# A two-layer encoder kernel on one core: the output projection's weight blocks are formed in another buffer, and four pieces of work around it change places

## The chip, the core and the metric

The kernel runs on one core of a Trainium2 chip. Its engines have queues of their own and run side by side: TensorE (PE in the profile: matmuls and transposes; PEld is its loading of weights), VectorE (DVE), ScalarE (ACT), GpSimd (POOL) and SyncE (SP, which only issues transfers). An instruction waits in its engine's queue until the semaphores it needs have come; what is queued behind it waits too. The metric is the device time of one execution, in microseconds (us).

## The reference

Two layers, each a gated mixer of three branches on 512 rows of 1024 numbers and then a SwiGLU FFN, all in float32. The part that the change is about:

```python
    merged = (g[:, :, 0] * jnp.einsum('bse,ed->bsd', o_a, w_branch_a[l])
              + g[:, :, 1] * jnp.einsum('bse,ed->bsd', o_b, w_branch_b[l])
              + g[:, :, 2] * jnp.einsum('bse,ed->bsd', o_c, w_branch_c[l]))
    mix = jnp.einsum('bsd,de->bse', merged, w_out[l])
    x = _layer_norm(DEEPNORM_ALPHA * x + mix, ln1_g[l], ln1_b[l])

    u = jnp.einsum('bsd,df->bsf', x, w_ffn_in[l])
    u_gate, u_up = jnp.split(u, 2, axis=-1)
    ffn = jnp.einsum('bsf,fd->bsd', jax.nn.silu(u_gate) * u_up, w_ffn_out[l])
    x = _layer_norm(DEEPNORM_ALPHA * x + ffn, ln2_g[l], ln2_b[l])
```

## The kernel before

**Products of pairs.** Each float32 operand is carried as a high part (a cast to float32r, on ACT) and a low part (the float32 number minus the high part, on DVE). One product is three matmuls onto one bank of PSUM: high by high, high by low, low by high (`mm3`, L121 to L124). For weights, `wh` and `wl` are the two parts and `st` is the float32 buffer that a transfer fills. There are four `st` buffers (NSTAGE), three `wh` and three `wl` (AHEAD), used in turn: a cast into `wh` waits until PE has finished the block that had the buffer three blocks earlier.

**Seven products instead of eight.** The large projections are done by Strassen-Winograd: the weights in four quarters W11, W12, W21, W22, the activations too, and seven products with sums of quarters on both sides. The kernel names the seven weight blocks m1, m2, y, v, x, g, h. A block has 1024 KB and is multiplied in two halves j (128 rows of the result each) by four k groups by three matmuls: 24 matmuls of 512 columns. The classes `Halves`, `Chain`, `Close`, `Early` and `Late` say how a block's weights come to be; `Staged` (L289) is one block: the cast at L297, the low part at L302. A quarter is added to another either by DVE (`tensor_add`) or by a transfer that POOL issues and that adds to what is in the buffer (`more`, L177). With `later=True` a block makes only its cast at once, and `low()` is called at another place.

**The output projection** (`out_items`, L1210) uses class `Late`. y's weights are W11 + W12, in buffer `a`. v's are W22, in buffer `d`. After v's two parts are made, DVE adds `a` into `d` (L247): these are x's weights. After x's parts, POOL adds W21 into `d` by a transfer (`more`, L282): h's weights. g's are W12 + W22, made by transfers in buffer `c` (`ahead_c`).

The activations of y and x are `s12` (left sums, `Quarters.left`), those of v and g `s43` (right sums, `Quarters.right`), those of m1 and m2 and h the merged rows. There are four such sums, k = 0 to 3, each two subtractions on DVE (L324 and L325, or L334 and L335), one cast on ACT (L108) and one low part on DVE (L114). Those of k = 2 and 3 are made while m2 and y run.

Each product ends in `plus` (L1192), which adds or subtracts its bank to the rows `z` of the residual stream (L1197 for the first addition to a piece of z, L1199 for the others). z has four row tiles t with two halves of 512 columns each. x, g and h go on in m1's banks: PE must not begin g in a bank until x's subtraction has read it, nor h until g's has. m1's and m2's additions are held back in the list `late` and made during v. When both halves of a row tile are complete, `normalise` (L515) computes mean and variance (bn_stats L499, aggregate L517), the reciprocal root on POOL (L520, a power) and the normalised rows (L522, two halves). x completes row tiles 0 and 1, h completes 2 and 3. Then PE transposes the rows (`transposes_of`, L540, into banks `px`), ACT applies gain and bias (L556), and xT's parts (L106, L112) are made from that. They are the activations of the FFN.

**The FFN's opening.** The first items are blocks m1 and m2 of w_ffn_in's first quarter set (`Chain`, object `ffn_opening`), then the plain tiles 16, 17, 18 (`u_ffn`; their weights are `Wt`, with casts and low parts in two halves of 1024 numbers, L154 and L155), then block y.

**What sets the order.** The program is a list of items; an item's weights are fetched (transfer, cast, low part) some items ahead (`run_items`, L585), and other work is put between an item's halves. From the traced program a scheduler with a priority for each instruction makes one order per engine at compile time. `tc.issue_after(ins)` forbids it to put an engine's instructions ahead of `ins` on the same engine; `behind[fn]` lists such instructions for what is fetched while item `fn` begins. Each engine runs its list in order.

Of the kernel before, what the change touches and what calls it, by code (L numbers as in the profile page):

```python
# [56 lines left out]
def trunk(ctx, tc, x_in, xT_in, w_in, ret_norm_g, da_norm_g, lq1, lk1, lq2, lk2, w_a, w_b, w_c, b_merge, w_out,  # L57
          ln1_g, ln1_b, w_ffn_in, w_ffn_out, ln2_g, ln2_b, rel, rope_ret, rope_da, decay, out):
    nc = tc.nc
# [131 lines left out]
    class Chain(Halves):  # L191
# [24 lines left out]
        def x(self):  # L216
            return self.take(1, 0)
# [3 lines left out]

        def v(self):
            return self.block(self.load(1, 1))

        def h(self):
            return self.block(self.__dict__.pop("a"))
# [50 lines left out]
    class Late(Early):  # L277


        def x(self):  # L280
            b = self.block(self.d)
            self.more(self.d, 1, 0)  # L282
            return b

        def h(self):
            self.closing = Staged(self.__dict__.pop("d"), self.kh, later=True)
            return self.closing
# [372 lines left out]
    def layer(l):  # L660
# [7 lines left out]
        v = {}  # L668
# [541 lines left out]
        def out_items():  # L1210
# [5 lines left out]
            def it(name, i, hf, op, last=False, whole=False):  # L1216
                def fn(wt):
                    on = {"x": "m1", "g": "m1", "h": "m1", "v": "y"}.get(name, name)
                    for j in range(2):
# [276 lines left out]
        p, q, r, u = u_fin(0, ffn_opening), u_fin(1, Close), u_fin(2, Close), u_fin(3, Close)  # L1496
        o, w = fout_items(0), fout_items(1)
        for (specs, fn), *groups in [
            (([ffn_opening.m1_high], p["m1"][1]), [], [s_turned(1)]), (p["m2"], [], [s_natural(0)]), (u_ffn(16), [s_x1(0)], [s_x1(1)]),
# [66 lines left out]
```

## Time and profile before

| | us |
|---|---|
| median of 3 runs (lowest, highest) | 1877.56 (1877.21, 1878.15) |
| profiled execution, its own time | 1878.1 |
| its span, first to last instruction | 1876.3 |
| PE busy | 1857.0 (99%) |
| DVE busy | 1392.5 (74%) |
| ACT busy | 989.6 (53%) |
| POOL busy | 129.9 (7%) |

Rows of the profile read: start, duration, engine, line, operation, output<-inputs, shape, and in brackets how long the engine was idle before and what ended that. In the table of waits the three numbers are the total, the number of times and the longest. In the table by stretches each engine has its busy time and its number of instructions, and behind them stand the granted PE clock, the share of the transfer engines and GB/s. Layer 0's output projection runs from about 553 to 596 us of the span, and the FFN's first blocks to 613; layer 1's lie 933.8 us later.

### The profile page before, as it was taken

The page shows a single profiled execution, that of the slowest core. Times are in us where ns is not written, and L with a number is a line of the kernel's source. Part 1 is how long each engine was busy: PE and PEld are TensorE (multiplying, and loading weights), DVE is VectorE, ACT ScalarE, POOL GpSimd, SP SyncE. Part 2 cuts the span into 40 slices and gives each one's busy share as a digit, 9 for nine tenths or more (in the row PEclk, how much of TensorE's full clock was granted, in tenths as well). Part 3 has the DMA queues.
Part 4 walks back from the last instruction along what each step waited for, and adds up shares of the span by engine and source line. Part 5 has one row for each costly group of instructions (what it writes and reads, how often), then busy time and mean ns, then how long its engine had stood idle before and what let it go on. Part 6 is the DMA issues. An engine that isn't in the chain of part 4 may idle for free.

```text
span 1876.3 us, 23363 instructions
## 1 busy us (share of the span) xinstructions
PE 1857.0 (99%) x8772; PEld 1546.9 (82%) x8772; DVE 1392.5 (74%) x2121; ACT 989.6 (53%) x1590; POOL 129.9 (7%) x151
## 2 busy tenths in 40 slices
PE   9999999999999999999999999999999999999998
PEld 7788888888887888888888888888888868888887
DVE  6777756677678776888687777567775887778886
ACT  5545545576545445555354555546665454455540
POOL 2000000000001000010010000000000011000100
PEclk9999999999999999999999999999999999999999
DMA  9685444332457577697486844433325486777871
GB/s 286 177 266 152 123 144 126 90 124 79 129 152 179 157 183 194 184 227 208 135 226 184 256 115 143 154 114 97 112 68 146 136 201 150 197 191 203 203 199 46
DMA packets 235425, 302.89 MB, mean 161 GB/s; under 512 B 8756, under 2 KB 127632, under 8 KB 235312
## 3 DMA queue, kind: packets, MB, share of 16 engines
q1 hardware_dynamic: 205888, 244.09, 40.0%
q0 software_dynamic: 29280, 57.05, 17.6%
q8 instruction: 69, 1.13, 0.2%
q14 instruction: 44, 0.36, 0.1%
q10 hardware_dynamic: 144, 0.26, 0.0%
HBM read 279.29 MB, written 22.07 MB: 161 GB/s over the span
## 4 chain that ended last, share of the span: by engine, by line
PE 88%; DVE 7%; ACT 2%; DMA 2%; issue 1%; POOL 0%; SPq 0%; DVEq 0%; ACTq 0%; POOLq 0%
PE pt L122 14%; PE pt L124 14%; PE pt L123 14%; PE pf L124 13%; PE pf L123 13%; PE pf L122 13%; DVE wl L302 2%; PE ptr L470 1%; ACT wh L297 1%; PE psc L441 1%; PE psc L440 1%; PE pco L983 1%; PE ph L1339 1%; DVE wl L155 1%; DMA xf<-in_xT 1%
## 5 line engine op out<-in xcount | busy, mean ns | idle before, releaser
L302 DVE TENSOR_TENSOR wl<-st,wh 128x2048 fp32r<-128x2048 f32 x140 | 320.2, 2290 | 119.9 <-ACT wh L297 119.3
L122 PE MATMUL pt<-xTh,wh 128*128 128x512 f32 x960 | 376.9, 393 | 1.3 <-ACT wh L154 0.7
L123 PE MATMUL pt<-xTl,wh 128*128 128x512 f32 x960 | 374.1, 390 | 0.4 <-DVE xTl L112 0.3
L124 PE MATMUL pt<-xTh,wl 128*128 128x512 f32 x960 | 374.1, 390 | 0.0
L297 ACT CAST wh<-st 128x2048 fp32r<-128x2048 f32 x140 | 267.1, 1912 | 199.9 <-PE pf L124 86.9
L154 ACT CAST wh<-st 128x1024 fp32r<-128x1024 f32 (+2 forms) x186 | 172.2, 949 | 121.8 <-PE pt L123 61.1
L155 DVE TENSOR_TENSOR wl<-st,wh 128x1024 fp32r<-128x1024 f32 (+2 forms) x186 | 200.6, 1096 | 46.1 <-ACT wh L154 32.4
L122 PEld LDWEIGHTS pt<-xTh,wh 128*128 128x128 f32 x960 | 180.2, 188 | 38.1 <-ACT wh L154 1.1
L124 PEld LDWEIGHTS pt<-xTh,wl 128*128 128x128 f32 x960 | 180.2, 188 | 38.0
L123 PEld LDWEIGHTS pt<-xTl,wh 128*128 128x128 f32 x960 | 180.4, 188 | 37.4 <-DVE xTl L112 0.7
L122 PE MATMUL pf<-wh,xTh 128*128 128x512 f32 x336 | 132.2, 395 | 0.4
L123 PE MATMUL pf<-wl,xTh 128*128 128x512 f32 x336 | 131.7, 392 | 0.6 <-DVE wl L302 0.6
L124 PE MATMUL pf<-wh,xTl 128*128 128x512 f32 x336 | 130.5, 391 | 0.0
L122 PE MATMUL pf<-wh,s43h 128*128 128x512 f32 x256 | 100.3, 393 | 2.0 <-DVE z L1199 2.0
L123 PE MATMUL pf<-wl,s12h 128*128 128x512 f32 x256 | 100.1, 391 | 1.2 <-DVE wl L302 1.2
L122 PE MATMUL pf<-wh,s12h 128*128 128x512 f32 x256 | 100.2, 395 | 0.0
L124 PE MATMUL pf<-wh,s12l 128*128 128x512 f32 x256 | 99.5, 390 | 0.0
L123 PE MATMUL pf<-wl,s43h 128*128 128x512 f32 x256 | 99.4, 390 | 0.0
L124 PE MATMUL pf<-wh,s43l 128*128 128x512 f32 x256 | 99.2, 390 | 0.0
L790 ACT COPY tc<-pf 128x512 f32<-128x512 f32 x84 | 48.5, 590 | 81.5 <-PE pf L124 78.2
L122 PEld LDWEIGHTS pf<-wh,xTh 128*128 128x128 f32 x336 | 63.2, 188 | 15.3 <-ACT xTh L106 1.4
L123 PEld LDWEIGHTS pf<-wl,xTh 128*128 128x128 f32 x336 | 63.4, 189 | 13.8 <-DVE wl L302 1.3
(328 smaller groups left out, 3668.1 us busy)
## 6 DMA issues: line engine op xcount, KB each, us to landing
st<-in_w_in SPq DMA_DIRECT2D x53, 1024.0 KB, 5.6
st<-in_w_ffn_in SPq DMA_DIRECT2D x38, 1024.0 KB, 5.8
st<-in_w_in SPq DMA_DIRECT2D x48, 512.0 KB, 4.8
st<-in_w_ffn_out SPq DMA_DIRECT2D x22, 1024.0 KB, 7.4
st<-in_w_ffn_in POOLq DMA_DIRECT2D x20, 1024.0 KB, 10.2
st<-in_w_ffn_out POOLq DMA_DIRECT2D x16, 1024.0 KB, 8.8
st<-in_w_in POOLq DMA_DIRECT2D x12, 1024.0 KB, 11.1
st<-in_w_ffn_in SPq DMA_DIRECT2D x24, 512.0 KB, 5.7
```

Of the source, the lines that this page charges most:

```text
L122: nc.tensor.matmul(ps, lh, rh, start=start, stop=False, skip_group_check=onto)
L123: nc.tensor.matmul(ps, lh, rl, start=False, stop=False, skip_group_check=onto)
L124: nc.tensor.matmul(ps, ll, rh, start=False, stop=stop, skip_group_check=onto)
L154: return [nc.scalar.copy(self.hi[:, a:b], self.st[:, a:b]), nc.vector.tensor_sub(self.lo[:, a:b], self.st[:, a:b], f(self.hi[:, a:b]))]
L155: nc.vector.tensor_sub(self.lo[:, a:b], self.st[:, a:b], f(self.hi[:, a:b]))]
L297: nc.scalar.copy(self.hi, st)
L302: nc.vector.tensor_sub(self.lo, self.st, f(self.hi))
L440: nc.tensor.matmul(ps[:, :w], self.q[j][:, n], self.k[j][:, :w], start=True, stop=False)
L441: nc.tensor.matmul(ps[:, :w], self.q[j][:, n], self.kl[j][:, :w], start=False, stop=True)
L470: nc.tensor.transpose(ps[:, o + P * (nt - mt):o + P * (nt - mt) + P], E[pk][:, c + P * mt:c + P * mt + P], ident)
L790: nc.scalar.copy(t[to, j], ps)
L983: nc.tensor.matmul(*x, start=mt == 0 and x is hi, stop=mt == NT - 1 and x is hi)
```

## The change

It has four parts, the same in both layers.

1. **x's weights on y's buffer.** `Late.v` adds `d` into `a` and no longer `a` into `d`. x, and then h, take their weights from `a`. The addition reads `d` and overwrites `a`, whose other readers are y's cast and low part.
2. **m2's sums around x.** The four held-back additions of m1 and m2 were made during v, m2's behind the last right sum's low part. Now m1's two and m2's first are made after v's first half, and m2's second after x's first half, behind the vector instruction ahead of x's own subtraction.
3. **g's cast behind the first right sum.** What is fetched when v and x begin stood, on DVE, behind the low part of the last right sum. It stands there still, and on ACT behind the cast of the right sum k = 2.
4. **FFN's second low part behind h.** Block m2 of the FFN makes only its cast when it is fetched; its low part is issued behind h's second addition. What is fetched when the FFN's m1 begins (tile 16's weights) stands, on DVE, behind the last normalisation.

```diff
@@ class Chain
+        def m2_high(self):
+            self.second = Staged(self.load(1, 0), self.kh, later=True)
+            return self.second
+
@@ class Late
+        def v(self):
+            d = self.load(1, 1)
+            b = self.block(d)
+            nc.vector.tensor_add(self.a, self.a, d)
+            return b
+
         def x(self):
-            b = self.block(self.d)
-            self.more(self.d, 1, 0)
+            b = self.block(self.a)
+            self.more(self.a, 1, 0)
             return b
 
+        def y(self):
+            return self.block(self.a)
+
         def h(self):
-            self.closing = Staged(self.__dict__.pop("d"), self.kh, later=True)
+            self.closing = Staged(self.__dict__.pop("a"), self.kh, later=True)
             return self.closing
@@ s_mright
                 mq[k].right(acc.pop(k), acc.pop(k + 4), 0.5)
+                if k == 2:
+                    proj["high"] = last_of(nc.scalar)
                 if k == 3:
-                    proj["sums"] = last_of(nc.vector)
                     for name in ("v", "x"):
-                        behind[proj[name][1]] = [proj["sums"]]
+                        behind[proj[name][1]] = [proj["high"], last_of(nc.vector)]
@@ out_items
-                        if name == "v":
-                            late[j]()
-                            with tc.issue_after(proj["sums"]):
-                                late[2 + j]()
+                        if name == "v" and j == 0:
+                            for _ in range(3):
+                                late.pop(0)()
+                        if name == "x" and j == 0:
+                            with tc.issue_after(last_of(nc.vector, 2)):
+                                late.pop()()
...
                             behind[proj["h"][1]] = [last_of(nc.vector)]
+                        if name == "h" and j == 1:
+                            with tc.issue_after(last_of(nc.vector)):
+                                ffn_opening.second.low()
                         if whole:
                             x1["n"].normalise(t)
+                        if name == "h" and j == 1:
+                            behind[proj["next"]] = [last_of(nc.vector)]
@@ the FFN's items
+        proj["next"] = p["m1"][1]
...
-(p["m2"], [], [s_natural(0)])
+(([ffn_opening.m2_high], p["m2"][1]), [], [s_natural(0)])
```

The number of instructions of each engine stays what it was, and the lists of SP and POOL keep their order. Those of DVE, ACT and PE change in these stretches alone. (After the change, lines behind L222 have other numbers: L302 becomes L315, L297 L310, L1197 L1211, L1199 L1213, L522 L535.)

DVE before, layer 0, while m2 and y run. st_4848 is `a`, st_5147 is `d`; wl_5150 is v's low part, wl_5188 x's; sa_5096 and sa_5103 are the left sums k = 2 and 3; z_4792 and z_4794 take m1's additions:

```order
L324 TENSOR_TENSOR sa_5096<-th_2515,th_3087 128x256
L1197 SCALAR_TENSOR_TENSOR z_4792<-z_4792,pf_5114 128x512
L325 TENSOR_TENSOR sa_5096<-sa_5096,th_2515 128x256
L1197 SCALAR_TENSOR_TENSOR z_4794<-z_4794,pf_5134 128x512
L302 TENSOR_TENSOR wl_5150<-st_5147,wh_5149 128x2048
L114 SCALAR_TENSOR_TENSOR s12l_5100<-sa_5096,s12h_5099 128x512
L324 TENSOR_TENSOR sa_5103<-th_2590,th_3162 128x256
L247 TENSOR_TENSOR st_5147<-st_5147,st_4848 128x2048
L325 TENSOR_TENSOR sa_5103<-sa_5103,th_2590 128x256
L302 TENSOR_TENSOR wl_5188<-st_5147,wh_5187 128x2048
```

The same place after:

```order
L337 TENSOR_TENSOR sa_5096<-th_2515,th_3087 128x256
L287 TENSOR_TENSOR st_4848<-st_4848,st_5147 128x2048
L338 TENSOR_TENSOR sa_5096<-sa_5096,th_2515 128x256
L315 TENSOR_TENSOR wl_5150<-st_5147,wh_5149 128x2048
L114 SCALAR_TENSOR_TENSOR s12l_5100<-sa_5096,s12h_5099 128x512
L337 TENSOR_TENSOR sa_5103<-th_2590,th_3162 128x256
L1211 SCALAR_TENSOR_TENSOR z_4792<-z_4792,pf_5114 128x512
L338 TENSOR_TENSOR sa_5103<-sa_5103,th_2590 128x256
L1211 SCALAR_TENSOR_TENSOR z_4794<-z_4794,pf_5134 128x512
L315 TENSOR_TENSOR wl_5188<-st_4848,wh_5187 128x2048
```

The addition moved ahead of v's low part, and m1's two additions to z moved behind it.

ACT before, from x's cast (wh_5187) over g's (wh_5220) to h's (wh_5256); s43h_5130 and s43h_5170 are the right sums k = 2 and 3:

```order
L297 CAST wh_5187<-st_5147 128x2048
L108 ACTIVATE s12h_5106<-sa_5103 128x512
L297 CAST wh_5220<-st_5007 128x2048
L108 ACTIVATE s43h_5130<-sb_5127 128x512
L108 ACTIVATE s43h_5170<-sb_5167 128x512
L297 CAST wh_5256<-st_5147 128x2048
```

The same place after (h's cast is now wh_5254):

```order
L310 CAST wh_5187<-st_4848 128x2048
L108 ACTIVATE s12h_5106<-sa_5103 128x512
L108 ACTIVATE s43h_5130<-sb_5127 128x512
L310 CAST wh_5220<-st_5007 128x2048
L108 ACTIVATE s43h_5170<-sb_5167 128x512
L310 CAST wh_5254<-st_4848 128x2048
```

g's cast and the first right sum's cast have changed places, and x and h read the other buffer.

DVE before, where h ends and the FFN begins. wl_5313 and wl_5416 are the low parts of the FFN's m1 and m2, wl_5463 that of tile 16; z_4796 and z_4798 take h's two additions; xTl are low parts of the FFN's activations:

```order
L302 TENSOR_TENSOR wl_5313<-st_5310,wh_5312 128x2048
L112 TENSOR_TENSOR xTl_5351<-xf_5352,xTh_5350 128x256
L302 TENSOR_TENSOR wl_5416<-st_5413,wh_5415 128x2048
L112 TENSOR_TENSOR xTl_5357<-xf_5358,xTh_5356 128x256
L1197 SCALAR_TENSOR_TENSOR z_4796<-z_4796,pf_5114 128x512
L1197 SCALAR_TENSOR_TENSOR z_4798<-z_4798,pf_5134 128x512
L499 BN_STATS bn_4810<-z_4796 128x6
L499 BN_STATS bn_4811<-z_4798 128x6
L112 TENSOR_TENSOR xTl_5368<-xf_5369,xTh_5367 128x256
L517 BN_AGGR mv_5433<-bn_4810 128x2
L517 BN_AGGR mv_5454<-bn_4811 128x2
L155 TENSOR_TENSOR wl_5463<-st_5461,wh_5462 128x1024
```

The same place after, from h's second addition (its first stands five rows further ahead, behind the first xTl) to the last normalisation:

```order
L1211 SCALAR_TENSOR_TENSOR z_4798<-z_4798,pf_5134 128x512
L532 TENSOR_SCALAR rs_5434<-mv_5432 128x1
L512 BN_STATS bn_4811<-z_4798 128x6
L535 TENSOR_SCALAR z_4796<-z_4796,mv_5432,rs_5434 128x512
L112 TENSOR_TENSOR xTl_5374<-xf_5375,xTh_5373 128x256
L535 TENSOR_SCALAR z_4797<-z_4797,mv_5432,rs_5434 128x512
L315 TENSOR_TENSOR wl_5416<-st_5413,wh_5415 128x2048
L112 TENSOR_TENSOR xTl_5385<-xf_5386,xTh_5384 128x256
L530 BN_AGGR mv_5454<-bn_4811 128x2
L532 TENSOR_SCALAR rs_5456<-mv_5454 128x1
L535 TENSOR_SCALAR z_4798<-z_4798,mv_5454,rs_5456 128x512
L112 TENSOR_TENSOR xTl_5391<-xf_5392,xTh_5390 128x256
```

h's additions and row tile 2's normalisation moved ahead of m2's low part; row tile 3's normalisation stands behind it, and tile 16's low part behind that.

More of the change, by code (lines that the diff above doesn't have):

```diff
@@ L1496, in layer @@
         p, q, r, u = u_fin(0, ffn_opening), u_fin(1, Close), u_fin(2, Close), u_fin(3, Close)
+        proj["next"] = p["m1"][1]
         o, w = fout_items(0), fout_items(1)
         for (specs, fn), *groups in [
-            (([ffn_opening.m1_high], p["m1"][1]), [], [s_turned(1)]), (p["m2"], [], [s_natural(0)]), (u_ffn(16), [s_x1(0)], [s_x1(1)]),
+            (([ffn_opening.m1_high], p["m1"][1]), [], [s_turned(1)]), (([ffn_opening.m2_high], p["m2"][1]), [], [s_natural(0)]), (u_ffn(16), [s_x1(0)], [s_x1(1)]),
             (u_ffn(17), [s_x1(2)], [s_x1(3)]), (u_ffn(18), [s_natural(1)], [s_x1r(0), p["c"]]), (p["y"], [s_x1r(1)], [s_x1r(2)]),
```

## The prediction

> **What bounds the kernel now.** I read the page first, then TensorE's (PE's) waits over the whole run, then the stretch that the change touches in each engine's rows.
>
> ```profile
> PE 1857.0 (99%) x8772; PEld 1546.9 (82%) x8772; DVE 1392.5 (74%) x2121; ACT 989.6 (53%) x1590; POOL 129.9 (7%) x151
> ...
> PE px L540 <- DVE z L522: 3.9, 2, 1.9
> PE pf L122 <- DVE z L1199: 2.0, 2, 1.0
> PE pf L123 <- DVE wl L302: 1.8, 4, 0.6
> ```
>
> PE is the bound, and what it waits for longest lies in the output projection and just behind it, once per layer. So only the idle PE time in these two stretches can be won. PE's rows of layer 0, then the same places in layer 1:
>
> ```profile
> 552.82 0.39 PE L122 MATMUL pf<-wh,m 128*128 128x512 f32 x1
> ...
> 558.26 0.39 PE L122 MATMUL pf<-wh,m2h 128*128 128x512 f32 x1
> ...
> 563.70 0.39 PE L122 MATMUL pf<-wh,s12h 128*128 128x512 f32 x1
> ...
> 570.28 0.50 PE L123 MATMUL pf<-wl,s12h 128*128 128x512 f32 x1 [0.60 <-DVE wl L302]
> ...
> 582.87 0.50 PE L122 MATMUL pf<-wh,s43h 128*128 128x512 f32 x1 [1.00 <-DVE z L1199]
> ...
> 589.45 0.47 PE L122 MATMUL pf<-wh,m2h 128*128 128x512 f32 x1 [0.32 <-DVE rs L519]
> ...
> 590.90 1.47 PE L540 MATMUL px<-ident,z 128*128 128x128 f32 x12
> 592.13 0.48 PE L122 MATMUL pf<-wh,m2h 128*128 128x512 f32 x1
> ...
> 604.37 0.80 PE L540 MATMUL px<-ident,z 128*128 128x128 f32 x4 [1.94 <-DVE z L522]
> ...
> 613.43 0.39 PE L122 MATMUL pt<-xTh,wh 128*128 128x512 f32 x1
> ```
> ```profile
> 1497.50 0.39 PE L122 MATMUL pf<-wh,s12h 128*128 128x512 f32 x1
> ...
> 1538.17 0.80 PE L540 MATMUL px<-ident,z 128*128 128x128 f32 x4 [1.95 <-DVE z L522]
> ...
> 1545.99 0.39 PE L122 MATMUL pt<-xTh,wh 128*128 128x512 f32 x1
> ```
>
> The blocks begin at 552.82 (m1), 558.26 (m2), 563.70 (y), 582.87 (g), 589.45 (h); 613.43 begins FFN tile 16. A block of 24 matmuls takes 558.26 - 552.82 = 5.44, so 0.227 each; twelve transposes take 592.13 - 590.90 = 1.23, 0.10 each. From y to tile 16 stand seven blocks (y, v, x, g, h, and m1 and m2 of the FFN: 168 matmuls, 38.1) and 32 transposes (3.3): 41.4. It takes 613.43 - 563.70 = 49.73 in layer 0 and 1545.99 - 1497.50 = 48.49 in layer 1: 8.4 and 7.1 are lost. That, 15.5, is the most that can be won. Layer 1 lies 933.80 behind layer 0, so that layer 0's times serve for both.
>
> **Why PE waits there.** The rows of VectorE (DVE), ScalarE (ACT) and GpSimd (POOL):
>
> ```profile
> 558.67 0.69 DVE L1197 SCALAR_TENSOR_TENSOR z<-z,pf 128x512 f32<-128x512 f32 x1
> ...
> 560.45 2.29 DVE L302 TENSOR_TENSOR wl<-st,wh 128x2048 fp32r<-128x2048 f32 x1 [0.15 <-ACT wh L297]
> ...
> 563.60 2.29 DVE L247 TENSOR_TENSOR st<-st 128x2048 f32<-128x2048 f32 x1
> ...
> 567.94 2.29 DVE L302 TENSOR_TENSOR wl<-st,wh 128x2048 fp32r<-128x2048 f32 x1 [1.72 <-ACT wh L297]
> ...
> 571.53 1.29 DVE L1197 SCALAR_TENSOR_TENSOR z<-z,pf 128x512 f32<-128x512 f32 x2
> 574.28 0.69 DVE L114 SCALAR_TENSOR_TENSOR s43l<-sb,s43h 128x512 fp32r<-128x512 f32 x1 [1.47 <-ACT s43h L108]
> ...
> 576.95 2.28 DVE L302 TENSOR_TENSOR wl<-st,wh 128x2048 fp32r<-128x2048 f32 x1
> ...
> 594.67 2.28 DVE L302 TENSOR_TENSOR wl<-st,wh 128x2048 fp32r<-128x2048 f32 x1
> ...
> 597.21 1.28 DVE L1197 SCALAR_TENSOR_TENSOR z<-z,pf 128x512 f32<-128x512 f32 x2
> ...
> 600.12 1.18 DVE L155 TENSOR_TENSOR wl<-st,wh 128x1024 fp32r<-128x1024 f32 x1
> ...
> 603.68 1.92 DVE L522 TENSOR_SCALAR z<-z,mv,rs 128x512 f32<-128x512 f32 x4 [0.46 <-POOL rs L520]
> ```
> ```profile
> 566.00 1.91 ACT L297 CAST wh<-st 128x2048 fp32r<-128x2048 f32 x1 [5.05 <-DVE st L247]
> ...
> 571.80 1.91 ACT L297 CAST wh<-st 128x2048 fp32r<-128x2048 f32 x1 [3.37 <-issue]
> 573.62 0.63 ACT L108 ACTIVATE s43h<-sb 128x512 fp32r<-128x512 f32 x1
> ...
> 580.78 3.71 ACT L297 CAST wh<-st 128x2048 fp32r<-128x2048 f32 x2 [4.47 <-DMA st<-in_w_out]
> ...
> 596.54 1.06 ACT L154 CAST wh<-st 128x1024 fp32r<-128x1024 f32 x1 [3.20 <-PE pf L124]
> ```
> ```profile
> 570.53 1.29 POOL L178 DMA_DIRECT2D st<-in_w_out  x1 [40.08 <-DMA st<-in_w_ffn_in]
> 587.02 0.57 POOL L520 TENSOR_TENSOR rs<-rs,mhalf 128x1 f32<-128x1 f32 x1 [15.20 <-DVE rs L519]
> ...
> 601.78 2.48 POOL L520 TENSOR_TENSOR rs<-rs,mhalf 128x1 f32<-128x1 f32 x2 [5.75 <-DVE rs L519]
> ```
>
> Two rows of 0.69 end after 1.29, so a DVE instruction starts about 0.09 before the printed end of the one ahead. The steps below use that.
>
> **1. x's weights on y's buffer.** The number of additions, transfers and casts is the same. Before, the addition (563.60) must stand behind v's low part (560.45), which reads the buffer that it overwrites; x's cast waits for it 5.05 (566.00) and x's low part 1.72 (567.94). Now it takes the slot of m1's z addition at 558.67 and ends at 560.96. v's low part goes to 561.2 to 563.5; its reader comes at 570.7. x's cast then waits only for m2's `wh`, free when m2's last matmul is through: 563.9 to 565.8. x's low part: 565.9 to 568.2, y's last low part until 568.8. PE now runs ten matmuls of y at 566.4 and reaches x's low part at 568.9 and y's last one at 569.4: no wait. v begins at 570.7, and the displaced z additions (0.69 each) stand at 564.3 and 565.3, where the addition was. It now needs v's weights at 558.7 instead of 560.4; these were asked for at 546.38, and such a load lands after 4.9:
>
> ```profile
> 546.38 0.37 SPq L174 DMA_DIRECT2D st<-in_w_out  x1
> ```
> ```profile
> st<-in_w_out SPq DMA_DIRECT2D x10, 1024.0 KB, 4.9
> ```
>
> **2. g's cast, and the sums.** Before, g's cast (571.80) stood ahead of the right sum's cast (573.62), so that DVE waited 1.47 at 574.28 and g's low part came at 576.95. Now the two right sums' subtractions end at 569.4, the cast is through at 570.1, and g's cast follows until 572.0. Low parts of the sums: 571.7 and 573.8; PE asks for them at 572.5 and 573.9, the second by 0.1 only. g's low part: 573.7 to 576.0. One of m2's additions stands ahead of it (0.60 in the chain), the other behind x's subtraction. That subtraction ends at 578.4. PE finishes x and wants to start g at 563.70 + 72 x 0.227 = 580.0, before 582.87: 2.85 won.
>
> **3. The accumulating transfer to h.** It is issued after x's low part, and 580.78 - 570.53 = 10.25 later h's cast begins. From 568.5 on that gives 578.75, the cast's end 580.7, h's low part 581.0 to 583.3 (2.29). The root of the variance is now asked for ahead of that low part. This is no free gain: with only bn_stats beside it POOL's power took 0.57 (587.02), behind a 1.18 low part (600.12 and the next) two took 2.48. I let it end at 583.7, behind h's low part. Two normalisations of 0.5, a bn_stats and the z subtraction that frees g's first bank then end at 586.0. PE is done with g and four transposes at 585.9. h begins at 586.05 instead of 589.45, another 0.55. Inside h the transposes wait 0.45 for the second row tile's normalisation; h ends at 593.25. Had POOL no such wait, 0.3 per layer more would be won.
>
> **4. The FFN's low part.** Before, m2's low part (594.67) and half a low part of tile 16 (600.12) stand ahead of h's additions (597.21) and of the last normalisations (603.68); that is PE's wait of 1.94. Now h's first addition runs at 591.6, ahead of m2's low part, and the first of the two normalisations is done at 596.3. The low part itself goes to 596.2 to 598.5, with the second aggregate, POOL's power and the second normalisation (600.2 to 601.0) behind it. m1 runs from 593.25 to 598.75. Its fourth k group needs an xTh that ACT casts only behind the cast of tile 16's first half (596.54: it waits for h's last matmul): at 594.8 against PE's 595.3, and its low part at 595.8 against 595.7. The first four transposes therefore begin at 598.75, not 604.37, and m2's low part is there. The next transposes wait 0.65 for the second normalisation. Tile 16's low parts (600.9 to 603.2) hide under m2. With 0.1 or so of restart after each of the waits, tile 16 begins at 606.9.
>
> **The clock.** In the same stretch of both layers:
>
> ```profile
> 604.30:609.20 4.90, 4.83 (x22) 4.24 (x23) 4.77 (x9) 4.28 (x11) 0.00 (x0) 0.65 1.21 291
> 1538.10:1543.00 4.90, 4.83 (x28) 3.67 (x29) 4.84 (x9) 4.33 (x11) 0.00 (x0) 1.00 1.21 292
> ```
>
> After nearly the same wait (1.94 and 1.95) the granted clock was 0.65 in layer 0 and 1.00 in layer 1; this makes the 1.24 between 49.73 and 48.49. With the longest wait at 0.65 I expect 1.00 in both. [...] The trace has the drop right behind the wait, so I follow the row.
>
> **The sum.** Layer 0: 613.43 - 606.9 = 6.5. Layer 1: 1545.99 - 933.80 = 612.2, less 606.9 = 5.3. Together 11.8. The profiled execution took 1878.1 (span 1876.3), 0.5 above the median of 1877.56; 1877.56 - 11.8 = 1865.8, say 1866. Nothing behind tile 16 takes it back: in the table of waits PE's other waits are all below 1 us, and the loads and POOL's transfers keep their order and are released by low parts that come earlier. The two half parts of tile 17 stand further back, some 6 us ahead of their use.
>
> **The rivals.**
> (a) The wait only moves: the normalisations stay late, because ACT's casts of xTh or POOL hold them up, and only steps 1 to 3 count: 2 x 3.4 = 6.8 less some new wait of 0.5 per layer gives 1872. For it: DVE has no idle time between 581 and 603 in my reckoning. Against: h's additions pass 3.5 us of low parts. Chance 0.13.
> (b) Slower: the transfer to h lands late. It is now on PE's path with 0.2 of room, h's cast, low part, power and subtraction behind it. Each us that it takes beyond 10.25 costs about 1 us per layer; beyond some 16 us it costs more than all that is won, and 20 would give 1866 + 2 x 9.75 = 1885. For it: the same queue's transfers share the engines with loads. Against: the same loads stand around it as before. Chance 0.03.
> (c) The order is changed but PE's waits are not, as other instructions were the last to come: within 1874 to 1881. The quoted releasers speak against it. Chance 0.06.
> The forecast has the remaining 0.78.
>
> **How the numbers follow.** The low end is all waits gone but 0.3 per layer: 1877.56 - 15.5 + 0.6 = 1862.7, say 1862.5. The high end takes in most of (a): 1871.5. Outside lie (b), (c) and a part of (a), under 0.2. A difference below 0.2% (3.75 us) can't be told from none. Faster: 0.78 + 0.13 and a little of (c), 0.92; same 0.05; slower 0.03.
>
> **What would show it.** Right: no wait of PE for `wl` L302 or for z between y and g; g's begin 16.3 behind y's; the addition on `st` ahead of v's low part; h's cast still behind a transfer; the wait for the last normalisation under 1 us; clock 1.00 in both layers. Wrong: a wait of PE for m2's low part or xTl in the FFN's first blocks, h's cast later than 15 us behind y's begin, or loads of tile 18 that come late.

## The result

The changed kernel takes 1865.98 us (median of 6 runs, 1865.59 to 1866.53) against 1877.56 (1876.59 to 1878.15) for the kernel before on the same chip: ratio 0.994, 95% interval 0.993 to 0.9951. It is faster by 11.6 us, and 1866 was forecast. Its profiled execution has a span of 1864.1.

### The profile after

PE's busy time on the page, and the head of the table of PE's waits (total, times, longest):

```profile
PE 1852.7 (99%) x8772; PEld 1547.0 (83%) x8772; DVE 1391.9 (75%) x2121; ACT 990.6 (53%) x1590; POOL 131.1 (7%) x151
```
```profile
PE warm L626 <- POOL ident masks.py:199: 1.5, 1, 1.5
PE pt L122 <- ACT wh L154: 0.7, 1, 0.7
PE px L553 <- DVE z L535: 0.7, 2, 0.4
```

The waits for z between y and g and for `rs` are gone from the table, those for `wl` fell from 1.8 in all to 0.2, and the wait for the last normalisation fell from 3.9 to 0.7 for both layers together. PE's rows at the same places as before, layer 0 and layer 1 (y, v, g, g's transposes, h, the FFN's m1, the two groups of transposes behind it, tile 16; of layer 1 only y and the last two):

```profile
563.21 0.39 PE L122 MATMUL pf<-wh,s12h 128*128 128x512 f32 x1
...
570.40 0.40 PE L122 MATMUL pf<-wh,s43h 128*128 128x512 f32 x1
...
579.72 0.39 PE L122 MATMUL pf<-wh,s43h 128*128 128x512 f32 x1
...
585.16 0.60 PE L553 MATMUL px<-ident,z 128*128 128x128 f32 x4
585.68 0.47 PE L122 MATMUL pf<-wh,m2h 128*128 128x512 f32 x1
...
592.79 0.39 PE L122 MATMUL pf<-wh,xTh 128*128 128x512 f32 x1
...
598.45 0.60 PE L553 MATMUL px<-ident,z 128*128 128x128 f32 x4
...
599.87 1.67 PE L553 MATMUL px<-ident,z 128*128 128x128 f32 x12 [0.35 <-DVE z L535]
...
606.44 0.39 PE L122 MATMUL pt<-xTh,wh 128*128 128x512 f32 x1
```
```profile
1490.40 0.39 PE L122 MATMUL pf<-wh,s12h 128*128 128x512 f32 x1
...
1527.14 1.67 PE L553 MATMUL px<-ident,z 128*128 128x128 f32 x12 [0.32 <-DVE z L535]
...
1533.72 0.39 PE L122 MATMUL pt<-xTh,wh 128*128 128x512 f32 x1
```

From y to tile 16 now take 606.44 - 563.21 = 43.23 in layer 0 and 43.32 in layer 1, where it was 49.73 and 48.49: 6.50 and 5.17 are won, 11.67 of the 12.2 by which the two profiled spans differ. Between the two stretches (tile 16 of layer 0 to y of layer 1) nothing moved: 883.96 after, 884.07 before. y itself begins 0.49 earlier (563.21 for 563.70), ahead of everything that was changed; 0.49 is therefore added below where times of layer 0 are held against the forecast.

The rows behind it, on VectorE, ScalarE and GpSimd:

```profile
558.18 2.29 DVE L287 TENSOR_TENSOR st<-st 128x2048 f32<-128x2048 f32 x1
...
560.72 2.29 DVE L315 TENSOR_TENSOR wl<-st,wh 128x2048 fp32r<-128x2048 f32 x1
...
565.41 2.29 DVE L315 TENSOR_TENSOR wl<-st,wh 128x2048 fp32r<-128x2048 f32 x1
...
573.33 2.28 DVE L315 TENSOR_TENSOR wl<-st,wh 128x2048 fp32r<-128x2048 f32 x1
...
580.59 2.28 DVE L315 TENSOR_TENSOR wl<-st,wh 128x2048 fp32r<-128x2048 f32 x1
583.34 1.00 DVE L535 TENSOR_SCALAR z<-z,mv,rs 128x512 f32<-128x512 f32 x2 [0.47 <-POOL rs L533]
...
595.68 2.28 DVE L315 TENSOR_TENSOR wl<-st,wh 128x2048 fp32r<-128x2048 f32 x1
...
599.27 0.55 DVE L535 TENSOR_SCALAR z<-z,mv,rs 128x512 f32<-128x512 f32 x1 [0.66 <-POOL rs L533]
```
```profile
577.76 1.91 ACT L310 CAST wh<-st 128x2048 fp32r<-128x2048 f32 x1 [5.08 <-DMA st<-in_w_out]
```
```profile
568.01 1.29 POOL L178 DMA_DIRECT2D st<-in_w_out  x1 [37.92 <-DVE wl L315]
...
580.75 2.55 POOL L533 TENSOR_TENSOR rs<-rs,mhalf 128x1 f32<-128x1 f32 x1 [11.46 <-DVE rs L532]
586.34 0.55 POOL L533 TENSOR_TENSOR rs<-rs,mhalf 128x1 f32<-128x1 f32 x1 [3.04 <-DVE rs L532]
```

The addition on `st` (558.18) stands ahead of v's low part (560.72), x's low part begins at 565.41 and g's at 573.33, h's cast (577.76) still waits for the transfer, POOL's power is held 2.55 beside h's low part, and m2's low part (595.68) stands ahead of the last row tile's normalisation (599.27).

### The profile page after: what moved, and what is told of

Its sections match the earlier page's. It is cut to its first block, busy times and chain, and to the rows that moved or that the text cites. A ratio compares the mean times of both kernels' runs of the same rounds, so it can differ in the third digit from the quotient of the medians.

```text
span 1864.1 us, 23351 instructions
## 1 busy us (share of the span) xinstructions
PE 1852.7 (99%) x8772; PEld 1547.0 (83%) x8772; DVE 1391.9 (75%) x2121; ACT 990.6 (53%) x1590; POOL 131.1 (7%) x151
## 5 line engine op out<-in xcount | busy, mean ns | idle before, releaser
L315 DVE TENSOR_TENSOR wl<-st,wh 128x2048 fp32r<-128x2048 f32 x140 | 320.3, 2291 | 117.4 <-ACT wh L310 116.8
L310 ACT CAST wh<-st 128x2048 fp32r<-128x2048 f32 x140 | 267.3, 1912 | 194.1 <-PE pf L124 100.3
L124 PEld LDWEIGHTS pf<-wh,xTl 128*128 128x128 f32 x336 | 63.1, 188 | 14.0 <-DVE xTl L112 0.7
```

The costliest lines, as they stand in the source:

```text
L124: nc.tensor.matmul(ps, ll, rh, start=False, stop=stop, skip_group_check=onto)
L310: nc.scalar.copy(self.hi, st)
L315: nc.vector.tensor_sub(self.lo, self.st, f(self.hi))
```

## The experiments

The theory is the prediction's: the four steps as priced, of which steps 1 to 3 (the parts 1 to 3) bring 3.4 per layer and step 4 (part 4) the rest. Tried against it are the prediction's rivals that the wait only moves (a) and that the transfer to h is close to the edge (b), and one more: that the parts hide one another. "y to tile 16" is the begin of tile 16's first matmul less that of y's first, in the profiled execution. Each ratio is to runs of the kernel before on the same chip. The rows come from several chips, on which the medians of before lie between 1876.82 and 1877.59; small differences between rows are therefore read from the last column.

| kernel | time (lowest to highest) | ratio, 95% interval | y to tile 16, layers 0 / 1 |
|---|---|---|---|
| changed | 1865.98 (1865.59 to 1866.53) | 0.9940 (0.9930 to 0.9951) | 43.23 / 43.32 |
| without part 1 | 1869.14 (1868.81 to 1870.13) | 0.9958 (0.9942 to 0.9975) | 44.70 / 44.59 |
| without part 2 | 1867.62 (1866.75 to 1868.94) | 0.9949 (0.9934 to 0.9964) | 43.82 / 43.81 |
| without part 4 | 1871.11 (1870.34 to 1871.33) | 0.9965 (0.9952 to 0.9979) | 44.98 / 46.52 |
| part 1 alone | 1871.09 (1870.65 to 1872.09) | 0.9967 (0.9955 to 0.9979) | 45.38 / 45.38 |
| part 2 alone | 1873.63 (1873.12 to 1873.98) | 0.9981 (0.9972 to 0.9990) | 46.97 / 46.93 |
| part 4 alone | 1873.84 (1872.96 to 1874.28) | 0.9981 (0.9972 to 0.9991) | 46.92 / 46.93 |
| transfer late, 512 columns | 1866.60 (1866.35 to 1867.16) | 0.9943 (0.9929 to 0.9958) | 43.27 / 43.29 |
| transfer late, 1536 columns | 1874.23 (1873.27 to 1874.88) | 0.9983 (0.9973 to 0.9992) | 47.24 / 47.24 |
| transfer behind the sums | 1879.49 (1878.85 to 1880.44) | 1.0011 (1.0002 to 1.0020) | 49.48 / 50.30 |
| root first | 1866.68 (1866.56 to 1867.16) | 0.9946 (0.9933 to 0.9958) | 43.56 / 43.56 |
| root first, cast held | 1865.36 (1865.28 to 1866.44) | 0.9939 (0.9925 to 0.9952) | 42.88 / 42.87 |
| both roots first | 1865.42 (1864.86 to 1865.80) | 0.9939 (0.9925 to 0.9952) | 42.80 / 42.79 |

Part 3 has no row of its own. With its lines undone, and parts 1, 2 and 4 in place, each engine's list is the same as in the changed kernel to the last row; and part 1 alone already puts g's cast behind the first right sum's cast. Part 3 asks for an order that part 1 brings about.

### Without part 4

```diff
-                        if name == "h" and j == 1:
-                            with tc.issue_after(last_of(nc.vector)):
-                                ffn_opening.second.low()
...
-                        if name == "h" and j == 1:
-                            behind[proj["next"]] = [last_of(nc.vector)]
...
-(([ffn_opening.m2_high], p["m2"][1]), [], [s_natural(0)])
+(p["m2"], [], [s_natural(0)])
```

> The changed kernel with part 4 undone: the FFN's m2 makes its low part when it is fetched again. If the prediction's steps hold, steps 1 to 3 stay (g 16.3 to 16.6 behind y, h 22.4 behind y) and only the stretch behind h falls back: PE waits some 1.9 for the last normalisation in both layers, y to tile 16 takes about 46.3 in layer 0 and 45.1 in layer 1, and the time is 1877.56 - 6.8 = 1870.8 (1869.5 to 1872). Rival A (the normalisations are set by DVE's queue and not by h's end): what steps 1 to 3 win is waited away, the wait grows to about 5 and the time is near 1877. Rival B (part 4 carries nothing, h's earlier end suffices): 1866. Clock: by the row of before a wait of 1.9 brings a halved stretch in at least one layer; if the wait does not bring it, there is none in either.

It took 1871.11, with g 16.5 and h 22.5 behind y. Behind h, PE waits for the normalisation in both layers:

```profile
600.66 0.81 PE L553 MATMUL px<-ident,z 128*128 128x128 f32 x4 [1.51 <-DVE z L535]
...
1530.00 0.80 PE L553 MATMUL px<-ident,z 128*128 128x128 f32 x4 [1.83 <-DVE z L535]
```

Rivals A and B fall: steps 1 to 3 keep their gain, and part 4 brings 5.1 more (1871.11 - 1865.98). Only the clock came out otherwise. The halved stretch stood in layer 1 (hence 46.52) and not in layer 0 (44.98), the other way round than in the kernel before. In the table by stretches (PE's busy time first, the granted clock third from the end), the two windows around each wait, first of the kernel before, then of this one:

```profile
602.12:605.54 3.42, 1.48 (x10) 0.91 (x9) 2.96 (x7) 2.75 (x4) 2.14 (x2) 1.00 1.15 294
605.54:608.95 3.41, 3.41 (x15) 3.12 (x14) 3.28 (x6) 3.11 (x8) 0.00 (x0) 0.50 1.21 290
1533.96:1537.38 3.42, 2.26 (x10) 1.42 (x8) 3.06 (x7) 2.04 (x5) 1.79 (x1) 1.00 1.10 231
1537.38:1540.79 3.41, 2.62 (x19) 2.31 (x20) 3.31 (x6) 2.84 (x7) 0.68 (x2) 1.00 1.20 304
```
```profile
598.91:602.33 3.42, 1.91 (x15) 1.42 (x14) 3.30 (x7) 3.02 (x5) 1.64 (x2) 1.00 1.15 294
602.33:605.74 3.41, 3.41 (x19) 2.47 (x18) 3.25 (x6) 3.41 (x10) 0.00 (x0) 1.00 1.21 290
1527.34:1530.75 3.41, 1.58 (x9) 0.93 (x7) 2.95 (x7) 2.54 (x4) 2.48 (x2) 1.00 1.13 279
1530.75:1534.16 3.41, 3.41 (x16) 3.25 (x15) 2.91 (x6) 2.53 (x8) 0.00 (x0) 0.50 1.21 290
```

The halved stretch lasts 3.41 in both (605.54 to 608.95 and 1530.75 to 1534.16), and in the two runs that have one in each layer (below) the stretches begin 931.84 apart, which is 273 x 3.4133. So I counted windows of that length from the one halved stretch of each execution. At the end of the span, where PE has finished, the clock is halved too, and that stretch begins a whole number of windows away: in the kernel before at 1871.88, 371 windows behind 605.54, and without part 4 at 1865.26, 98 windows behind 1530.75. In the kernel before, layer 0's wait of 1.94 falls into one window, which is then busy for 1.48 of 3.41, and the next is halved. Layer 1's wait of 1.95 lies across two of them (busy 2.26 and 2.62), and nothing is halved. Without part 4, layer 1's window, with a wait of 1.83, is busy 1.58 (the next is halved) and layer 0's, with the shorter wait of 1.51, 1.91 (the next is not). PE's busy time in such a window does not settle it in every case: in the run with both roots first (below) the window that holds the last matmuls (1854.28 to 1857.69) was busy 1.57, and the next one had the full clock. That the place of the wait among these windows decides is my reading of these cases; no run tried it by itself.

### Part 4 alone

```diff
+            self.second = Staged(self.load(1, 0), self.kh, later=True)
...
+                                ffn_opening.second.low()
...
+                            behind[proj["next"]] = [last_of(nc.vector)]
```

> The kernel before with part 4 alone. If the steps add up: the waits at x (0.6) and g (1.0) stay, g 19.2 behind y, but the wait for the last normalisation is under 1 and the clock is 1.00 in both layers: 2 x 1.9 plus 1.24 of the clock, 1877.56 - 5.0 = 1872.5 (1871.5 to 1874). Rival: with h's weights late DVE is too full behind h, m2's low part is then waited for by PE in its place, and the time stays within 1875.5 to 1878.

It took 1873.84, in the upper part of the first range; the waits at x and g stayed (0.59 and 0.98), the last wait is 0.35, and the clock is 1.00. Between y and tile 16 it wins 48.49 - 46.93 = 1.56 in layer 1, where before had no halved stretch, less than the 1.9 of step 4. Here too ScalarE has two casts of tile 17's weights ahead of the activations (38.32 and 39.57 behind y), where the changed kernel has one; what they cost here was not separated. The rival falls.

### Without part 1, and part 1 alone

```diff
-        def v(self):
-            d = self.load(1, 1)
-            b = self.block(d)
-            nc.vector.tensor_add(self.a, self.a, d)
+        def x(self):
+            b = self.block(self.d)
+            self.more(self.d, 1, 0)
             return b
...
-            self.closing = Staged(self.__dict__.pop("a"), self.kh, later=True)
+            self.closing = Staged(self.__dict__.pop("d"), self.kh, later=True)
```

`Late` again uses the `v` that it inherits, which adds `a` into `d` (L247 of the kernel before).

> The changed kernel with part 1 undone: x's weights are added onto v's buffer again, the other three parts stay. By step 1 and step 3 of the prediction x's low part comes 2.0 later, PE waits for it as before (some 0.8 to 1.1 per layer between y and g), the transfer to h is issued 2.0 later, h's low part ends near 585.3 and h begins 1.4 to 2.0 later than 586.05: 1866 + 2 x 1.4 to 2 x 2.0 = 1868.8 to 1870. Rival: the other parts hide it, since g's cast and the sums were the bound: 1866 to 1867.

It took 1869.14, within the range. PE waits for x's low part again (0.59), g begins 17.67 behind y (16.51 in the changed kernel) and h 23.76 (22.47): 1.2 and 1.3 more in layer 0.

> The kernel before with part 1 alone. The order that results has g's cast behind the first right sum's cast already, so this is steps 1 and 3 without part 2 and part 4. By the steps: no wait at x, g begins 0.6 to 1.2 later than with all parts but 1.7 to 2.2 earlier than before, the wait for the last normalisation stays near 1.9: 1870.8 + 1.2 to 2.4 = 1872 to 1873.2. Rival: without part 2 the wait at g stays as it was and only the 0.9 to 1.1 per layer at x are won: 1875.4 to 1875.8.

This came out faster than I thought: 1871.09, as without part 4 (1871.11). g began 16.52 behind y and h 22.62, near the 16.51 and 22.47 with all parts. Part 2 is therefore not needed for g's begin once part 1 has brought the low parts, and with them g's cast, forward, and what separates this kernel from the changed one lies behind h.

### Part 2 alone, and without part 2

```diff
-                        if name == "v":
-                            late[j]()
-                            with tc.issue_after(proj["sums"]):
-                                late[2 + j]()
+                        if name == "v" and j == 0:
+                            for _ in range(3):
+                                late.pop(0)()
+                        if name == "x" and j == 0:
+                            with tc.issue_after(last_of(nc.vector, 2)):
+                                late.pop()()
```

> The kernel before with part 2 alone: m2's additions to z split around x. By the steps the sums' low parts and g's low part are late because of ACT's order and of x's late cast, which stay, so nothing or little is won: 1876.5 to 1878. Rival: DVE's rows ahead of x's subtraction are the whole of the wait at g (1.0): 2 x 0.6 to 2 x 1.0 are won, 1875.5 to 1876.4.

More was won than in either expectation: 1873.63. Alone, part 2 brings g 1.18 forward (17.99 behind y in place of 19.17), and the last wait falls apart into two of 0.81 and 0.50 from one of 1.94, while the wait at h grows from 0.32 to 0.80. So parts 1 and 2 are each a remedy for the wait at g, and their gains overlap: 5.9 (part 1 alone), 3.4 (part 2 alone) and 3.4 (part 4 alone) against each one's runs of before make 12.7, together they bring 11.6.

> The changed kernel with part 2 undone: m2's two additions to z stand behind the last right sum's low part again. By step 2 up to two more instructions of 0.60 in the chain stand ahead of x's subtraction, so g begins 0.6 to 1.2 later and PE waits there for z: 1866 + 1.2 to 2.4 = 1867.2 to 1868.4. Rival: they fall into DVE's idle time, g begins where it does now: 1866.0 (within 0.5). Other rival: g waits 1.0 and h with it as before, 2 x 2.85 are lost: 1871.7.

1867.62 lies in the range, but for another reason than the one given. g begins 16.51 behind y, exactly as in the changed kernel, so no time is lost at x's subtraction. The 0.6 per layer (43.82 for 43.23) is lost between the second transposes and tile 16. There two casts of half of tile 17's weights stand ahead of the activations, instead of one:

```profile
598.25 1.05 ACT L154 CAST wh<-st 128x1024 fp32r<-128x1024 f32 x1 [1.84 <-PE pf L124]
599.21 0.40 ACT L106 CAST xTh<-xf 128x256 fp32r<-128x256 f32 x1
599.51 1.04 ACT L154 CAST wh<-st 128x1024 fp32r<-128x1024 f32 x1
600.46 1.01 ACT L569 ACTIVATE xf<-px,colv 128x256 f32<-128x256 f32 x2
```

Whether this pair of casts is the cause was tried on the next kernel, which has it too.

### The root first, and the cast held

```diff
                         if name == "x" and j == 1:
-                            with tc.issue_after(last_of(nc.vector, 2)):
+                            with tc.issue_after(proj["first"]):
                                 hv.closing.low()
...
                         if whole:
                             x1["n"].normalise(t)
+                            if name == "x" and j == 0:
+                                proj["first"] = last_of(nc.vector)
```

`proj["first"]` is the last VectorE instruction of row tile 0's normalisation.

> The changed kernel with h's low part behind the first row tile's normalisation and no longer ahead of it, so that POOL's power runs without a two-operand DVE instruction beside it. By step 3 (POOL was held behind h's low part): the power takes 0.55 in place of 2.55, the second row tile's normalisation ends about 0.8 earlier, the wait inside h (0.45) goes and nothing takes its place: 0.3 to 0.45 per layer, 1866 - 0.6 to 0.9 = 1865.1 to 1865.4. Rival: h's low part, 1.7 later, is now what h's first matmuls wait for, or the subtraction that frees g's bank is: 1866 to 1868.

The mechanism was right and the time was not: 1866.68. With h's low part behind the first normalisation POOL's power is short (2.55 in the changed kernel):

```profile
580.98 0.58 POOL L533 TENSOR_TENSOR rs<-rs,mhalf 128x1 f32<-128x1 f32 x1 [11.47 <-DVE rs L532]
```

The FFN's m1 begins 29.21 behind y in place of 29.58: 0.37 is won, and 0.45 in layer 1. But tile 16 begins 43.56 behind y, 0.33 later than in the changed kernel (0.24 in layer 1), and two casts of tile 17 stand ahead of the activations on ScalarE. Behind the second transposes PE stops twice where the changed kernel does not, 0.18 for a high part of the activations and 0.12 for a low part (in the second row, the weight load that waited for it):

```profile
602.37 0.50 PE L122 MATMUL pf<-wh,xTh 128*128 128x512 f32 x1 [0.18 <-ACT xTh L106]
...
603.46 0.19 PEld L124 LDWEIGHTS pf<-wh,xTl 128*128 128x128 f32 x1 [0.43 <-DVE xTl L112]
```

In the next kernel tile 17's casts are held behind the activations' last cast:

```diff
+                if hf == 1:
+                    behind[proj["second"]] = [last_of(nc.scalar)]
...
+        proj["second"] = p["m2"][1]
```

> The run root_first with one thing more: the casts of tile 17's weights are held on ScalarE behind the last cast of the FFN's activations, of which one stood ahead of them in the changed kernel and two in root_first. If those casts (1.05 each) are what took back the 0.37 that root_first won at h, y to tile 16 takes at most 43.23 - 0.37 = 42.9 in both layers in place of 43.56, and the time is 1866.68 - 1.4 = 1865.3 or less. Rival: VectorE's low parts of tiles 16 and 17, which stand between the low parts of the activations, are the bound; then it stays at 43.5 and 1866.7.

y to tile 16 fell to 42.88 and 42.87 and the time to 1865.36, as expected, and both stops are gone. So it was tile 17's weights that took the gain back, and not the low parts of tile 16, which still stand between those of the activations on VectorE (36.96 and 38.43 behind y). The casts alone are not shown to be it: with them tile 17's two low parts, at 39.89 and 41.70 behind y in root first, left this stretch of VectorE as well. For the casts speaks the wait for ScalarE's xTh, and that tile 17's low parts stood behind the xTl that PE waited for last.

### Both roots first

```diff
+                            behind[proj["next"]] = [last_of(nc.vector)]
                             with tc.issue_after(last_of(nc.vector)):
                                 ffn_opening.second.low()
```

These lines stand behind the last normalisation here, in addition to the edit of root first; the casts are not held.

> As the run before it, and the FFN m2's low part behind the last normalisation too. By step 4: the wait of 0.35 for the last normalisation goes as well; the low part ends near 599.1 and PE, with sixteen transposes ahead of m2, asks for it near 600: 0.6 to 0.8 per layer in all, 1864.4 to 1864.8. Rival: the low part comes behind PE's request, PE waits for m2's low part in place of the normalisation: 1866 to 1867.

1865.42, y to tile 16 42.80 and 42.79. All sixteen transposes run in one piece without a wait:

```profile
598.08 1.91 PE L553 MATMUL px<-ident,z 128*128 128x128 f32 x16
```

It wins 0.43 and 0.53 of the 0.6 to 0.8 expected per layer; a wait of 0.16 for a low part of the activations (xTl) has come in m2. The times of this and of the cast-held kernel are 0.6 below the changed kernel's, which is less than these runs can separate; in the traces both layers agree.

### The transfer to h

```diff
+            s = self.a.rearrange("p k c -> p (k c)")[:, :512]
+            nc.gpsimd.tensor_scalar_add(s, s, 0.0)
             self.more(self.a, 1, 0)
```

The second run has `:1536` in place of `:512`.

> The changed kernel with one POOL instruction more per layer, behind x's low part and ahead of the accumulating transfer to h: it adds 0 to a fourth of x's weights (128 x 512), so the transfer is issued later by its length d, to be read in the trace. The prediction (rival b): room 0.2, then 1 us per us and layer: 1866 + 2 x (d - 0.2). Reading the trace of the changed kernel, h's low part (580.59) began 0.9 behind its cast's end (579.67), so that the room may be 0.9: 1866 + 2 x (d - 0.9). Rival: the transfer is hidden behind other work and d of 1 to 2 costs nothing: 1866.

The transfer was issued 6.76 behind y in place of 4.80, and nothing was lost: 43.27 and 43.29. Neither formula holds. The rows of layer 0:

```profile
568.31 1.86 POOL L293 TENSOR_SCALAR st<-st 128x512 f32<-128x512 f32 x1 [37.64 <-DVE wl L317]
570.47 1.32 POOL L178 DMA_DIRECT2D st<-in_w_out  x1 [0.30 <-POOL st L293]
581.28 0.58 POOL L535 TENSOR_TENSOR rs<-rs,mhalf 128x1 f32<-128x1 f32 x1 [9.48 <-DVE rs L534]
```

In layer 0 h's low part now waits 0.42 for its cast, so the power (581.28) runs ahead of it and takes 0.58 in place of 2.55; in this kernel and in the changed one VectorE comes to the normalisation at the same time, 20.1 behind y. In layer 1 it was the transfer that made up for the delay: 8.62 from issue to cast, where the changed kernel had 9.36, so that low part (17.4 behind y) and power (2.55) stand as they did.

> As the run with 512, with three times the columns (128 x 1536), so that d is two to three times as long. The prediction: 1866 + 2 x (d - 0.2), with room 0.9 1866 + 2 x (d - 0.9); both give the same slope between the two runs, 2 us of time for 1 us of d. Rival: nothing is lost, 1866. Clock: PE would then wait more than 1.5 us at h or its first transposes; by the row of before such a wait can halve the clock in a layer, and 1.2 to 1.7 more would be lost there; if waits of this length do not do it, the clock stays 1.00.

This run did not test what it was made for. The instruction on POOL took 4.45, and the VectorE instruction that fell beside it, 0.42 in the changed kernel (568.22), took 3.44:

```profile
569.33 3.44 DVE L349 TENSOR_TENSOR sb<-th,sa 128x256 f32<-128x256 f32 x1
```

The right sums were late by that, v waited 2.09 in both layers, and behind it the clock was 0.50 in both (574.43 to 577.85 and 1506.27 to 1509.68). The transfer was issued 4.6 later behind y, but g itself began 4.0 later, so its room was hardly touched. Of the 4.0 lost per layer, 2.09 are the wait and, by estimate, 3.41 / 2 = 1.71 the halved stretch; 0.2 are left over. To hold the transfer back without POOL:

```diff
+        def g(self):
+            s = self.a[:, 0, 0:1]
+            nc.vector.tensor_scalar_add(s, s, 0.0)
+            self.more(self.a, 1, 0)
+            return super().g()
```

> The changed kernel with the accumulating transfer to h held back by data and not by POOL: it is issued when g is fetched, behind a VectorE instruction that adds 0 to one column of x's weights and stands behind the last right sum's low part. It should be issued near 10.1 behind y's begin in place of 4.8, so 5.3 later, with nothing added on POOL. By the prediction's rival (b), room 0.2 and then 1 us per us: h begins 5.1 later, 27.6 behind y. From the run with 512 columns, where 2.0 later cost nothing because the root of the variance then got POOL to itself: room 1.7, h begins 3.6 later, 26.1 behind y. If the transfer is hidden: 22.5. PE then waits 3.6 to 5.1 at h in both layers. If the clock halves whenever about half of a 3.41 window is idle, it halves once in each layer (1.7 more each): 1866 + 2 x (3.6 + 1.7) = 1876.6 with room 1.7, 1879.6 with room 0.2; if it does not halve, 1873.2 and 1876.2.

```profile
574.39 1.29 POOL L178 DMA_DIRECT2D st<-in_w_out  x1 [43.87 <-issue]
```
```profile
588.55 0.89 PE L557 MATMUL px<-ident,z 128*128 128x128 f32 x4 [2.85 <-DVE z L539]
590.28 0.77 PE L122 MATMUL pf<-wh,m2h 128*128 128x512 f32 x1 [0.84 <-DVE mv L534]
```

Issued 10.8 behind y (y begins at 563.59), 6.0 later than in the changed kernel, it delays h to 26.69 behind y, by 4.22; in layer 1 by 4.03. If each us beyond the room costs one, as rival (b) has it, the room is 1.8 to 2.0. The run with 512 columns fits that, since 1.96 later cost nothing there. So rival (b) has the edge too near; its slope fits both runs, but no run between the two tries it by itself. In layer 0 the 6.0 shrink step by step: h's cast is 5.7 later behind y (the transfer took 9.4), its low part 4.8 (VectorE came to it 0.9 after the cast before), the normalisation behind it 4.2 (POOL's power, 0.58 at 581.14, now runs ahead of the low part at 585.74). The clock was 0.50 for 3.41 in layer 0 (590.24 to 593.65) and for twice that in layer 1 (1522.08 to 1528.90). With the estimate of 1.7 for each 3.41, 2 x 4.1 + 3 x 1.7 = 13.3, and 1879.49 - 1865.98 = 13.5. All of the gain is then gone: 1879.49 against 1877.59 for before (ratio 1.0011, 1.0002 to 1.0020).

## Why the prediction was right, and where it was not

**The bound and the sum.** Right. Nearly all of the gain lies between y and tile 16, 6.50 and 5.17 against 6.5 and 5.3, and nothing behind takes it back. That the time met the forecast to 0.2 is luck in part: the sum takes all of layer 0's halved stretch (1.24) off a median of runs of which, by those beside the experiments, only about half had one (see the clock, below), and two small errors cancel (h 0.12 late, the last wait 0.30 shorter).

**Step 1.** Right to 0.2: in the forecast's frame x's low part began at 565.90 (forecast 565.9) and v at 570.89 (570.7). Undone, it costs 1.47 and 1.27 between y and tile 16, or 1.6 per layer by the times.

**Step 2.** The times are right (g's low part at 573.82 for 573.7, g at 580.21 for 580.0), the attribution is not. That m2's divided additions are needed for g's begin is refuted by the kernel without part 2, where g begins the same 16.51 behind y; that g's cast needs part 3 is refuted by the identical lists. Parts 1 and 2 overlap here. The 0.6 per layer that part 2 still brings is won behind h; by the runs above, most likely through where the scheduler puts the second half of tile 17's weights.

**Step 3.** The begin of h is right (586.17 for 586.05), and so is POOL held behind h's low part (its power took 2.55 beside it, and 0.58 in root first without it). The transfer took 9.75 (9.36 in layer 1) and not 10.25 from issue to cast. "0.2 of room" is wrong: by the two runs that delayed the transfer it is 1.8 to 2.0. Two things were overlooked. VectorE does not come to h's low part before 0.9 after the cast is through; and when the low part comes later the power gets ahead of it, so that the normalisation follows the low part at once, without the 0.47 that VectorE waited for POOL. That freeing POOL wins 0.3 per layer is right up to the FFN's m1 (0.37), and was lost again behind the second transposes, with tile 17's weights.

**Step 4.** Right in its places (m2's low part at 596.17 for 596.2, tile 16 at 606.93 for 606.9); the last wait was 0.35 and not 0.65. Its size without the clock is 1.56 in layer 1 by the kernel with part 4 alone, for 1.9; undone from the changed kernel it costs 1.75 in layer 0, where neither had a halved stretch.

**The clock.** Right that the drop goes with the wait: up to the last matmul no stretch below 1.00 was found here, with a longest wait of 0.35 in this part, and drops came only in runs with waits of 1.8 and more. But I took the 1.24 for a property of layer 0. Waits of 1.83 to 1.96 for the last normalisation brought a drop in two cases and none in three: the profiled execution with part 1 alone waited 1.96 and 1.95 and had no drop in either layer. That agrees with the reading by windows: counted back from its last halved stretch (1863.96), the windows with those waits were busy 1.89 in layer 0, and 2.90 and 1.97 in layer 1. The 1.24 belongs to the profiled execution, and the runs of before carry it only in part. Of the 14 beside the first four experiments, 7 have a mean granted clock of 0.998 and took 1877.37 to 1878.83, and 7 have 0.999 and took 1876.17 to 1877.00. All 6 runs of the changed kernel have 0.999 and spread over 0.9.

**The rivals.** (a) did not happen: without part 4 steps 1 to 3 gave 1871, and part 4 went on top. Its price of 1872 lay just outside the high end of 1871.5, which was said to take in most of it. (b) is real: with the transfer issued 6.0 later all of the gain was gone; but the edge is not where the prediction put it. (c) did not happen.

## What to carry to other kernels

Price a gain per wait and not per part of an edit: two parts can cure the same wait, and a third can ask for an order that is there already, which only undoing each shows. Behind a scheduler, compare the lists of all engines after each small edit, since half of a weight tile (a cast of 1.04 and the low part behind it) that slipped ahead of what PE waits for took back nearly twice what the edit had won. A wait of about 2 us can cost more than its length, but in some executions only: behind 1.94 the clock was halved for 3.41 here, behind 1.95 it was not.

## What the runs showed of the hardware

- The halved stretches up to the last matmul lasted 3.41 each, or twice that in one case, and the first ones of two layers began 931.84 = 273 x 3.4133 apart. Windows of that length, at full clock, in which PE was busy 0.70 to 1.58 (six: 1.48 in the kernel before, 1.58 without part 4, 1.32 and 1.32 with the transfer late by 1536 columns, 0.88 and 0.70 with the transfer behind the sums) were followed by a halved one; those read with 1.89 and more were not; one with 1.57, at the very end of a span, was not either. In the run with the transfer behind the sums, a halved window busy for 2.82 was followed by a second halved one, one busy for 3.37 by full clock:

```profile
1522.08:1525.49 3.41, 2.82 (x8) 1.81 (x8) 3.34 (x9) 0.59 (x1) 0.56 (x1) 0.50 0.84 242
1525.49:1528.90 3.41, 3.41 (x14) 3.01 (x13) 3.41 (x4) 1.21 (x3) 0.00 (x0) 0.50 0.30 71
```

- POOL and VectorE instructions took longer side by side: in the changed kernel a power took 2.55 where it began (580.75) just behind a low part of 2.28 (580.59), and 0.55 at 586.34, beside no low part. A VectorE instruction of 0.42 took 0.83 beside a POOL instruction of 1.86 (512 columns), and 3.44 beside one of 4.45 (1536 columns): 2.6 longer for 2.6 longer.
